# The convolution's second product by tokens, and a written order behind gate and up, in a trunk kernel on one core

## The chip, the cores and the metric

The kernel runs on one core of a Trainium2 chip. The metric is the device time of one launch in microseconds. The engines are named as the profile names them: PE is TensorE's matmul queue and PEld its weight loads, DVE is VectorE, ACT is ScalarE, POOL is GpSimd, SP is SyncE, which here only starts DMAs.

## The reference, cut to what matters

One sequence of 256 tokens with 2048 features (in float32) goes through a convolution layer, a feed-forward of width 5632, one dilated attention layer with shared keys and values, a second feed-forward and a last norm. The change touches the end of the convolution layer and both feed-forwards:

```python
def _conformer_conv(h, w1, b1, dw, dw_b, ln_g, ln_b, w2, b2):
    u = h @ w1 + b1
    a, gate = jnp.split(u, 2, axis=-1)
    u = a * jax.nn.sigmoid(gate)
    u = lax.conv_general_dilated(...) + dw_b      # 31 taps, causal, by feature
    u = jax.nn.silu(_layernorm(u, ln_g, ln_b))
    return u @ w2 + b2

h = h + _conformer_conv(_rmsnorm(h, a_norm_g), ...)
h = h + _swiglu(_rmsnorm(h, ffn_norm_g[0]), w_gate, w_up, w_down)   # (silu(x @ wg) * (x @ wu)) @ wd
```

In the kernel, `z` is the normed and activated input of the product with w2, `hT` the residual h, `x` the input of the following product.

## The kernel before, in words

**Products in three passes.** A float32 product is worked out from two parts of each operand, a rounded high part and the remainder: high by high, high by low, low by high. ACT rounds a weight block (`whi`), DVE or POOL subtracts (`wlo`). Blocks come from HBM by SP's DMAs (`raw`, 512 KB, three buffers), two blocks ahead of use (`emit_block`, `next_block`).

**Two layouts.** *By features*: a 128 x 128 tile of the weight is stationary, the activation moves; `project` and `group` run a wide pass of 512 columns (256 tokens, high and low) and a narrow one of 256. The result has features on partitions. *By tokens*: a tile of the activation is stationary (128 tokens), 512 columns of the weight move, three matmuls of 512 for each pair of k tile and token half (`nat`, called by `two_blocks`). The result has tokens on partitions.

**Couples by seven products.** By tokens, two k tiles, two token halves and two blocks of 512 columns make a 2 x 2 by 2 x 2 block product; an item "S" does it in 7 products instead of 8, from sums of the weights (`emit_sums`, on DVE), sums of the activation (`sum_up`) and four extra banks that `combine` adds up. An item "n" is a plain pair of k tiles for both column blocks. The order of items for a product is a string, such as "nnSnSnSn".

**Around the change.** The convolution layer goes over 16 feature tiles j, 12.5 us each: product with w1 (units u, four blocks each), gate, then the taps, shared among DVE, ACT, POOL and, for the last two tiles, PE. POOL also makes w1's low parts. Behind it stands LayerNorm, whose mean and variance come from PE (`st`), then square root on ACT and reciprocal on DVE (line 721). `centred`, `scaled` and `parted` (lines 697 to 710) make z tile by tile: subtract the mean, multiply, Silu on ACT, then cast to the high part and subtract for the low part. This stands in a `manual_schedule`, that is, ACT, DVE and POOL run in the order written. Elsewhere a scheduler sets the order on each engine ahead of the run; `in_order` and `tc.issue_after` pin an instruction behind another on its engine.

The product with w2 is by features: `project_pair` (lines 399 to 421) does the first two units, with the first four k tiles as native float32 matmuls (line 406) so that it can start before z is cast; `out_proj` does the other six and adds bias and residual (`residual`), sums squares (`Norm.add`, on ACT and POOL) and makes the next x from hT (`split_scaled`). The first feed-forward needs the residual by tokens, so it turns hT by 32 transposes (`turn_over`, line 838) and makes the norm's factor for tokens by eight small matmuls (`Norm.rstd_nat`, line 485).

The output product of the attention (wo) is already by tokens: `out_tokens` adds the product to the token-wise residual, sums squares on ACT (`Tokens.add`) and, through `x_of` and `turn_tiles` (line 876), turns each block of 512 features into x, using the product's own banks. `later(n, fn)` runs fn at the n+1-th following `tick`; a tick is one block of weights.

**Gate and up.** `ffn_hidden` goes over 11 couples of column blocks. Behind each, `hidden` (line 968) adds the combined banks to gate and up on DVE (lines 972, 975), runs Silu on ACT (line 973), multiplies on DVE (line 976), and `turned` (line 986) transposes the result for the down product. Their place among the weight splits is the scheduler's, the splits alone (`split`, line 250) are in a written chain.

[...] By tokens, `first_banks` (three `aux`, one `one`) and `second_banks` (two double `pp`) alternate as the plain banks and as the extra banks of the couples.

Of the kernel before, what the change touches and what calls it, by code (L numbers as in the profile page):

```python
# [9 lines left out]
F32 = mybir.dt.float32  # L10
# [6 lines left out]
P = 128  # L17
D = 2048
S = 256
# [34 lines left out]
SUMS_O, REST_O = 3, (0, 1)  # L54

# [3 lines left out]
for _n, _w in (("a_g", DT), ("b1", 2 * DT), ("dw", DT * TAPS), ("dw_b", DT), ("ln_g", DT), ("ln_b", DT),  # L59
               ("b2", DT), ("kv_g", DT), ("b_g", DT), ("f0_g", DT), ("f1_g", DT), ("eps", 2)):  # L60
    _VEC[_n] = _NV
    _NV += _w
# [34 lines left out]
def trunk(ctx: ExitStack, tc: tile.TileContext, xT, vec, const, w1, w2, wk, wv, wq, wo, wg0, wu0, wd0, wg1, wu1, wd1, fing, out):  # L97
# [126 lines left out]
    last_split = {}  # L224

# [50 lines left out]
    def emit_block():  # L276
# [7 lines left out]
        native = NATIVE if g == 0 and (w is w1 or w is w2 and u < 2) else 0  # L284
# [11 lines left out]
        for s in range(0, gk, step):  # L296
            if with_x:
                load_x(GK * g + s, step)
            part = slice(s, s + step)
            nc.sync.dma_start(raw[:, part, :], src[:, part, :])  # L300
            part = slice(max(s, native), s + step)
            if natural:
                split(hi, lo, raw)
                continue
            if part.start < part.stop:
                nc.scalar.copy(hi[:, part, :], raw[:, part, :])  # L306
                eng = nc.gpsimd if (w is w1 and u > 1) or (w is w2 and u < 2 and (u, g) in ((0, 1), (1, 1), (0, 2))) else nc.vector
                eng.tensor_tensor(out=lo[:, part, :], in0=raw[:, part, :], in1=hi[:, part, :].bitcast(F32), op=ALU.subtract)  # L308
# [90 lines left out]
    def project_pair(w, xf, x, bks):  # L399

        parts = [next_block(w, u, 0, 0)[0] for u in range(2)]
        for s in range(0, GK, 2):
            for bk, raw in zip(bks, parts):
                for kt in (s, s + 1):
                    for m in range(2):
                        nc.tensor.matmul(bk[:, m, 0, :], raw[:, kt, m * P:(m + 1) * P], xf[:, kt, :], start=kt == 0, stop=False,
                                         skip_group_check=True)
            yield
        for g in range(1, DT // GK):
            for u, bk in enumerate(bks):  # L410
                hi, lo = next_block(w, u, g, 0)[1:]
                tiles = [(g * GK + j, j, m, slice(m * P, (m + 1) * P)) for j in range(GK) for m in range(2)]
                for wide in ((True, False), (False, True))[u]:
                    for kt, j, m, ws in tiles:
                        if not wide:
                            nc.tensor.matmul(bk[:, m, 0, :], lo[:, j, ws], x[:, kt, 0, :], start=False, stop=False, skip_group_check=True)
                        else:
                            nc.tensor.matmul(bk[:, m, :, :], hi[:, j, ws], x[:, kt, :, :], start=False, stop=kt == DT - 1,
                                             skip_group_check=True)
                yield  # L420

    def nat(jobs, stop=False):

        for o, xs, hi, _, start in jobs:
            nc.tensor.matmul(o, xs[0], hi, start=start, stop=False, skip_group_check=True)  # L425
            nc.tensor.matmul(o, xs[1], hi, start=False, stop=False, skip_group_check=True)  # L426
# [64 lines left out]
    def residual(bk, u, bias, norm):  # L491

        h2 = hT[:, 2 * u:2 * u + 2, :]
        if bias is None:
            nc.vector.tensor_tensor(out=h2, in0=bk[:, :, 0, :], in1=h2, op=ALU.add)
        else:
            for i in range(2):
                nc.vector.scalar_tensor_tensor(out=h2[:, i, :], in0=bk[:, i, 0, :], scalar=v(bias, 2 * u + i), in1=h2[:, i, :],
                                               op0=ALU.add, op1=ALU.add)
        nc.vector.tensor_tensor(out=h2, in0=bk[:, :, 1, :], in1=h2, op=ALU.add)  # L500
        norm.add(h2)

    def out_proj(w, kt_n, x, bias, g, first=()):

        nx = joined_x()
        norm = Norm()
        for u in range(DT // 2):
            residual(first[u] if u < len(first) else project(w, u, kt_n, x), u, bias, norm)
            for i in (2 * u, 2 * u + 1):
                split_scaled(nx, i, v(g, i))  # L510
        return nx, norm


# [4 lines left out]
    with tc.tile_pool(name="cv", bufs=1) as cv, tc.tile_pool(name="cvu", bufs=1) as cvu:  # L518
# [139 lines left out]
        for j in range(DT):  # L658
            if j != 1:
# [21 lines left out]
        for _ in range(3):  # L681
            emit_block()
# [7 lines left out]
        bks = [bank2(), bank2()]  # L690
        pair = project_pair(w2, cT, z, bks)
        with tc.manual_schedule(engines={mybir.EngineType.Activation, mybir.EngineType.DVE, mybir.EngineType.Pool}):
            mu = cv.tile([P, S], F32, name="mu", tag="shift")
            rl = sp.tile([P, S], F32, name="rstd")
            groups = [(0, 1), (1, 1)] + [(j, 2) for j in range(2, DT, 2)]

            def centred(j, n, eng, m):
                c2 = cT[:, j:j + n, :]
                eng.tensor_tensor(out=c2, in0=c2, in1=_bc(m, n), op=ALU.subtract)

            def scaled(j, n):

                c2 = cT[:, j:j + n, :]
                nc.vector.tensor_tensor(out=c2, in0=c2, in1=_bc(st[:, 1, :], n), op=ALU.mult)
                for q in range(j, j + n):
                    nc.scalar.activation(cT[:, q, :], cT[:, q, :], AF.Silu, bias=v("ln_b", q), scale=v("ln_g", q))

            def parted(j, n):
                nc.vector.tensor_copy(z[:, j:j + n, 0, :], cT[:, j:j + n, :])
                nc.vector.tensor_tensor(out=z[:, j:j + n, 1, :], in0=cT[:, j:j + n, :], in1=z[:, j:j + n, 0, :].bitcast(F32), op=ALU.subtract)  # L710


            nc.scalar.activation(rl, st[:, 0, :], AF.Square)
            nc.scalar.copy(mu, st[:, 0, :])
            centred(*groups[0], nc.vector, st[:, 0, :])
            nc.vector.tensor_tensor(out=rl, in0=st[:, 1, :], in1=rl, op=ALU.subtract)
            nc.scalar.activation(rl, rl, AF.Sqrt, bias=ln_eps)
            centred(*groups[1], nc.vector, st[:, 0, :])
            for j, n in groups[5:]:
                centred(j, n, nc.gpsimd, mu)  # L720
            nc.vector.reciprocal(st[:, 1, :], rl)
            for i, (j, n) in enumerate(groups):
                if 2 <= i < 5:
                    centred(j, n, nc.vector, st[:, 0, :])
                scaled(j, n)
                if j in (1, 2):
                    next(pair)
                if j >= 8:
                    parted(j - 4, 2)
                if j == 10:  # L730
                    next(pair)
                    next(pair)
            emit_block()
            parted(12, 2)
            next(pair)
            parted(14, 2)
            next(pair)
            emit_block()
            emit_block()
            next(pair)  # L740
            next(pair)
            parted(0, 2)
            parted(2, 2)

        x, norm = out_proj(w2, DT, z, "b2", "f0_g", bks)


    def first_banks():

        b = [aux([P, NBV]) for _ in range(3)]  # L750
        return [b[0], b[2]], [b[1], one.tile([P, NBV], F32, name="b", tag="one")]

    def second_banks():
        b = [[a[:, i, :, :].rearrange("p a b -> p (a b)") for i in range(2)] for a in (bank2(), bank2())]
        return [[b[i][t] for i in range(2)] for t in range(2)]

    def wide(a):
        return a.rearrange("p (a b) -> p a b", b=P)

    def sum_up(sums, u, two, h, d):  # L760

        h, d = h.rearrange("p (a b) -> p a b", b=S), wide(d)
        two = two.bitcast(F32)
        nc.vector.tensor_tensor(out=h, in0=two[:, :, 0, :], in1=two[:, :, 1, :], op=ALU.add)
        a11, a21, a12, a22 = (h[:, j, t * P:(t + 1) * P] for j in range(2) for t in range(2))
        for i, a, b, op in ((0, a21, a22, ALU.add), (1, d[:, 0, :], a11, ALU.subtract), (2, a11, a21, ALU.subtract),
                            (3, a12, d[:, 1, :], ALU.subtract)):
            nc.vector.tensor_tensor(out=d[:, i, :], in0=a, in1=b, op=op)
        nc.scalar.copy(sums[:, u, :, 0, :], d)
        nc.vector.tensor_tensor(out=sums[:, u, :, 1, :], in0=d, in1=sums[:, u, :, 0, :].bitcast(F32), op=ALU.subtract)  # L770

    n_used = [0]

    def two_blocks(a, b, items, n_sums, n_rest, act, sums, cs, sum_banks, combine):


        u_sums, u_plain = pairs_of(items, n_sums)
        ab = a, b
# [485 lines left out]
```

## Time and profile before

| what | value |
|---|---|
| median of 3 runs (lowest, highest) | 2128.96 us (2127.24, 2130.54) |
| the profiled execution: its time, its span | 2130.14 us, 2128.4 us |
| convolution layer up to LayerNorm | about 0 to 223 us |
| product with w2 | 229 to 322 us |
| first gate and up | 322 to 797 us |
| product with wo | 1318 to 1409 us |
| second gate and up | 1409 to 1883 us |
| HBM traffic | 194 GB/s over the span |

A row of a timeline or chain starts with its start and its length in microseconds; `x3` merges three instructions; in square brackets stands the engine's idle time before it and what ended it. Matmuls overlap in their pipeline, so a matmul's own duration is longer than the distance from one to the next; that distance is what counts. The page's groups end with busy time, mean nanoseconds of one, and the engine's idle time before them.

### The profile page before, as it was taken

To read this page: it belongs to the slowest core of one execution; us is meant where nothing else is said; L and a number is where in the kernel's file an instruction comes from. 1 tells how busy PE (TensorE), PEld (TensorE's weight loads), DVE (VectorE), ACT (ScalarE), POOL (GpSimd) and SP (SyncE) were. 2 spreads that over 40 slices of the span, in tenths; PEclk is the share of its full clock that TensorE was granted. 3 is DMA by queue.
4 is the path that set the end of the run, shared out by engine and by line. 5 is a ranking of instruction groups with operands and counts; after the bars stand their busy time and mean duration, and the time that the engine had idled before them with its cause. 6 is when DMAs were issued, how large, how long until landed. Compare 5 with 4: busy or idle time off the path is not lost.

```text
span 2128.4 us, 28467 instructions
## 1 busy us (share of the span) xinstructions
PE 2103.3 (99%) x10316; PEld 1775.7 (83%) x10316; DVE 1780.6 (84%) x2431; ACT 1186.4 (56%) x1563; POOL 349.6 (16%) x350
## 2 busy tenths in 40 slices
PE   8999899999999999999999999999999999999998
PEld 8999788888888888888888888888888888878886
DVE  6888876888998998878895687887998899888877
ACT  6665555555555555555654566565555555555453
POOL 5999110000000100000000100000000000000200
PEclk9999999999999999999999999999999999999999
DMA  7555367555655557565656645565655565566664
GB/s 246 186 159 169 97 182 239 177 196 198 209 187 198 198 195 250 189 217 190 224 191 194 215 159 160 196 217 182 212 185 195 197 208 188 198 218 211 208 208 149
DMA packets 116095, 414.84 MB, mean 195 GB/s; under 512 B 13041, under 2 KB 14065, under 8 KB 115953
## 3 DMA queue, kind: packets, MB, share of 16 engines
q1 hardware_dynamic: 84960, 301.82, 43.5%
q0 software_dynamic: 30272, 110.11, 14.9%
q8 instruction: 81, 1.33, 0.3%
q10 hardware_dynamic: 720, 1.07, 0.1%
q14 instruction: 62, 0.50, 0.1%
HBM read 404.57 MB, written 8.39 MB: 194 GB/s over the span
## 4 chain that ended last, share of the span: by engine, by line
PE 87%; DVE 6%; DMA 3%; ACT 2%; issue 2%; POOL 0%; SPq 0%; DVEq 0%; ACTq 0%; POOLq 0%
PE pp L425 11%; PE pp L429 10%; PE pp L426 10%; PE aux L425 9%; PE aux L429 9%; PE aux L426 9%; PE pp L352 7%; PE pp L393 7%; PE pp L356 4%; PE b L429 2%; PE b L425 2%; PE b L426 2%; DVE wlo L250 2%; DVE rooms L259 1%; ACT whi L248 1%
## 5 line engine op out<-in xcount | busy, mean ns | idle before, releaser
L250 DVE TENSOR_TENSOR wlo<-raw,whi 128x1024 fp32r<-128x1024 f32 x360 | 431.5, 1229 | 101.4 <-ACT whi L248 86.4
L248 ACT CAST whi<-raw 128x1024 fp32r<-128x1024 f32 x360 | 369.6, 1050 | 254.8 <-DMA raw<-wd 86.7
L306 ACT CAST whi<-raw 128x1024 fp32r<-128x1024 f32 (+1 forms) x189 | 194.4, 1035 | 169.8 <-PE pp L352 55.1
L248 ACT CAST whi<-rooms 128x1024 fp32r<-128x1024 f32 (+1 forms) x140 | 144.9, 1038 | 219.5 <-DVE rooms L259 184.4
L308 DVE TENSOR_TENSOR wlo<-raw,whi 128x1024 fp32r<-128x1024 f32 (+1 forms) x144 | 177.0, 1245 | 79.7 <-ACT whi L306 65.6
L425 PE MATMUL pp<-whi,x 128*128 128x512 f32 x513 | 201.1, 392 | 0.0
L426 PE MATMUL pp<-whi,x 128*128 128x512 f32 x513 | 199.7, 389 | 0.0
L250 DVE TENSOR_TENSOR wlo<-rooms,whi 128x1024 fp32r<-128x1024 f32 (+1 forms) x140 | 168.4, 1203 | 11.1 <-ACT whi L248 7.6
L239 POOL DMA_DIRECT2D work<-wu x60 | 33.1, 551 | 780.5 <-DVE rooms L259 732.6
L425 PE MATMUL aux<-whi,x 128*128 128x512 f32 x404 | 159.0, 394 | 0.0
L426 PE MATMUL aux<-whi,x 128*128 128x512 f32 x404 | 157.4, 390 | 0.0
L250 DVE TENSOR_TENSOR wlo<-work,whi 128x1024 fp32r<-128x1024 f32 x120 | 114.4, 954 | 42.9 <-ACT whi L248 42.3
L429 PE MATMUL pp<-wlo,x 128*128 128x512 f32 x513 | 149.0, 389 | 0.0
L582 DVE SCALAR_TENSOR_TENSOR aux<-up,vecs,aux 128x256 f32<-128x256 f32 x350 | 140.9, 481 | 1.5 <-ACT aux L580 1.5
L248 ACT CAST whi<-work 128x1024 fp32r<-128x1024 f32 x120 | 95.7, 832 | 75.9 <-DMA work<-wg 36.3
L429 PE MATMUL aux<-wlo,x 128*128 128x512 f32 x404 | 132.5, 390 | 0.5 <-DVE wlo L250 0.5
L425 PEld LDWEIGHTS pp<-whi,x 128*128 128x128 f32 x513 | 96.3, 188 | 22.6 <-DVE hid L989 2.9
L425 PE MATMUL pp<-whi,hid 128*128 128x512 f32 x292 | 113.8, 390 | 1.3 <-DVE hT L842 1.3
L426 PE MATMUL pp<-whi,hid 128*128 128x512 f32 x292 | 113.6, 389 | 0.0
L429 PEld LDWEIGHTS pp<-wlo,x 128*128 128x128 f32 x513 | 96.3, 188 | 20.1
L426 PEld LDWEIGHTS pp<-whi,x 128*128 128x128 f32 x513 | 96.3, 188 | 19.7
L393 PE MATMUL pp<-x,whi 128*128 128x256 f32 x600 | 111.9, 288 | 0.0
(378 smaller groups left out, 5022.5 us busy)
## 6 DMA issues: line engine op xcount, KB each, us to landing
raw<-wd SPq DMA_DIRECT2D x128, 512.0 KB, 4.3
raw<-wg SPq DMA_DIRECT2D x116, 512.0 KB, 4.2
raw<-wu SPq DMA_DIRECT2D x116, 512.0 KB, 3.9
raw<-w SPq DMA_DIRECT2D x75, 512.0 KB, 3.8
work<-wg POOLq DMA_DIRECT2D x60, 512.0 KB, 4.6
work<-wu POOLq DMA_DIRECT2D x60, 512.0 KB, 3.8
t<-wd POOLq DMA_DIRECT2D x48, 512.0 KB, 4.4
raw<-wk SPq DMA_DIRECT2D x32, 512.0 KB, 4.1
```

What stands on the lines that cost most here:

```text
L239: nc.gpsimd.dma_start(places[0][:, 1:3, :], src[1])
L248: made.append(nc.scalar.copy(hi, raw))
L250: made.append(nc.vector.tensor_tensor(out=lo, in0=raw, in1=hi.bitcast(F32), op=ALU.subtract))
L306: nc.scalar.copy(hi[:, part, :], raw[:, part, :])
L308: eng.tensor_tensor(out=lo[:, part, :], in0=raw[:, part, :], in1=hi[:, part, :].bitcast(F32), op=ALU.subtract)
L352: nc.tensor.matmul(bk[:, m, :, :], hi, x[:, k, :, :], start=k == 0, stop=k == kt_n - 1 and turned, skip_group_check=True)
L356: nc.tensor.matmul(bk[:, m, 0, :], lo, x[:, k, 0, :], start=False, stop=k == kt_n - 1 and not turned, skip_group_check=True)
L393: nc.tensor.matmul(bks[u][:, m, :], a[:, j, m * P:(m + 1) * P], b, start=kt == 0 and m == 0 and i == 0, stop=kt == DT - 1 and i == len(pas ...
L425: nc.tensor.matmul(o, xs[0], hi, start=start, stop=False, skip_group_check=True)
L426: nc.tensor.matmul(o, xs[1], hi, start=False, stop=False, skip_group_check=True)
L429: nc.tensor.matmul(o, xs[0], lo, start=False, stop=stop and last[id(o)] == n, skip_group_check=True)
L582: nc.vector.scalar_tensor_tensor(out=acc[i % 2], in0=win, scalar=w, in1=acc[i % 2], op0=ALU.mult, op1=ALU.add)
```

## The change

1. The product with w2 is by tokens: w2 is laid out in blocks of two k tiles by 512 columns, `out_tokens` does it, the first half of the columns with plain items only, the second half with three couples by seven products. The first three blocks' low parts are made on POOL, the others by `split` on DVE.
2. The residual is by tokens from the start: late in the convolution, hT's buffer is filled anew with x by tokens (`xN`, two SP DMAs at j = 9), and b2, spread over the tokens, is added by two accumulating DMAs from POOL at j = 11. The first feed-forward is called with `by_tokens` true and so turns nothing over.
3. z: tiles 0 to 3 in a written order, the rest from the queue of `later`, two tiles every second tick; the reciprocal is copied out of PSUM (`rs`), so that its bank can be used.
4. `nat` does all products with the high activation, then all with the low one. `x_of` does all eight transposes, then the scaling; it runs at `later(2 + 2 * i)` instead of `later(1 + i)`, in the product with wo too.
5. `hidden`: the four sums, the Silus and the products are put into the written chains of DVE and ACT that hold the weight splits.

`sum_up` and the sums' places only change form. The helper functions between `first_banks` and `residual_back` move up in the file.

```diff
+ITEMS_2 = "nnnnnnnn", "nnSnSnSn"
+SUMS_2, REST_2 = 3, (0, 1)
...
-    for g in range(DT // GK):
-        blocks.extend((w2, u, g, GK) for u in range(2))
-    for u in range(2, DT // 2):
-        plan(w2, u, DT)
+    for pair, items in enumerate(ITEMS_2):
+        plan_two((w2, 2 * pair), (w2, 2 * pair + 1), items, items.count("S"), REST_2[pair])
...
-        native = NATIVE if g == 0 and (w is w1 or w is w2 and u < 2) else 0
+        native = NATIVE if g == 0 and w is w1 else 0
+        if w is w2:
+            natural = first_w2[0] <= 0
+            first_w2[0] -= 1
...
-                eng = nc.gpsimd if (w is w1 and u > 1) or (w is w2 and u < 2 and (u, g) in ((0, 1), (1, 1), (0, 2))) else nc.vector
-                eng.tensor_tensor(out=lo[:, part, :], in0=raw[:, part, :], in1=hi[:, part, :].bitcast(F32), op=ALU.subtract)
+                eng = nc.gpsimd if w is w1 and u > 1 or w is w2 else nc.vector
+                made = eng.tensor_tensor(out=lo[:, part, :], in0=raw[:, part, :], in1=hi[:, part, :].bitcast(F32), op=ALU.subtract)
+                if eng is nc.gpsimd:
+                    on_pool.append(made.ins)
...
         for o, xs, hi, _, start in jobs:
             nc.tensor.matmul(o, xs[0], hi, start=start, stop=False, skip_group_check=True)
+        for o, xs, hi, _, start in jobs:
             nc.tensor.matmul(o, xs[1], hi, start=False, stop=False, skip_group_check=True)
...
     def x_of(nx, c, banks, g):
-        for j, b in enumerate(banks):
-            b = turn_tiles(c, j, b)
+        for j, b in enumerate([turn_tiles(c, j, b) for j, b in enumerate(banks)]):
             for a in range(2):
...
-                later(1 + i, lambda c=c, banks=[cs[t][i] for t in range(2)]: x_of(nx, c, banks, lambda j: v(g, j)))
+                later(2 + 2 * i, lambda c=c, banks=[cs[t][i] for t in range(2)]: x_of(nx, c, banks, lambda j: v(g, j)))
...
         def hidden(c, cs, summed):
+            if summed:
+                for i in range(2):
+                    for t in range(2):
+                        with in_order("DVE") as made:
+                            made.append(nc.vector.tensor_tensor(out=q[t][i], in0=cs[t][i], in1=q[t][i], op=ALU.add))
+            for t in range(2):
+                g, r = q[t][0], norm.rn[:, t:t + 1]
+                with in_order("ACT") as made:
+                    made.append(nc.scalar.activation(g, g if summed else cs[t][0], AF.Silu, scale=r))
+                silu.append(made[-1].ins)
+            def product():
+                for t in range(2):
+                    (g, u), r = q[t], norm.rn[:, t:t + 1]
+                    with in_order("DVE") as made:
+                        made.append(nc.vector.scalar_tensor_tensor(out=u, in0=u if summed else cs[t][1], scalar=r, in1=g, op0=ALU.mult, op1=ALU.mult))
+            product()
...
         for j in range(DT):
+            if j == 9:
+                hT = rp.tile([P, DT, S], F32, name="hT", tag="hT")
+                for t in range(2):
+                    nc.sync.dma_start(hT[:, :, t * P:(t + 1) * P], xN[t].rearrange("p (k n) -> p k n", n=P))
+            if j == 11:
+                for t in range(2):
+                    with tc.issue_after(on_pool[-1]):
+                        nc.gpsimd.dma_start(hT[:, :, t * P:(t + 1) * P], b2.rearrange("p (k n) -> p k n", n=P), accum_op=ALU.add)
...
-        for _ in range(3):
-            emit_block()
+        emit_block()
...
             nc.vector.reciprocal(st[:, 1, :], rl)
+            scaled(0, 1, st[:, 1, :])
+            scaled(1, 1, st[:, 1, :])
+            scaled(2, 2, st[:, 1, :])
+            parted(0, 1)
+            parted(1, 1)
+            nc.vector.tensor_copy(rs, st[:, 1, :])
+            begun = parted(2, 2).ins
             emit_block()
+        def prepared(j):
+            with tc.issue_after(begun):
+                if j > 4:
+                    centred(j, 2, nc.vector, mu)
+                scaled(j, 2, rs)
+                parted(j, 2)
+        for j in range(4, DT, 2):
+            later(max(0, j - 6), lambda j=j: prepared(j))
+        for k in range(SUMS_2):
+            later((11, 14, 17)[k], lambda k=k: sum_up(sums, k, z[:, 2 * k:2 * k + 2, :, :], room("sq"), room("sq")))
+        later(12, lambda: load_first_sums(w2, four, *pieces))
+        x, norm = out_tokens(w2, ITEMS_2, REST_2, z, sums, "f0_g", 0)
...
-        hid = ffn_hidden(ff, scratch, wg0, wu0, x, norm, False, 0)
+        hid = ffn_hidden(ff, scratch, wg0, wu0, x, norm, True, 0)
...
+        "xN": np.ascontiguousarray(x[0].reshape(2, P, D)),
+        "b2": np.ascontiguousarray(np.broadcast_to(conv_b2[0], (P, D))),
-        "w2": _blocks(conv_w2[0]),
+        "w2": _blocks(conv_w2[0], GKV, NBV),
```

More of the change, by code (lines that the diff above doesn't have):

```diff
@@ L503, in out_proj, with first_banks, second_banks @@
[L503 to L510, printed above, removed]
-        return nx, norm
+    def first_banks():
+        b = [aux([P, NBV]) for _ in range(3)]
+        return [b[0], b[2]], [b[1], one.tile([P, NBV], F32, name="b", tag="one")]
+    def second_banks():
+        b = [[a[:, i, :, :].rearrange("p a b -> p (a b)") for i in range(2)] for a in (bank2(), bank2())]
+        return [[b[i][t] for i in range(2)] for t in range(2)]
@@ L689, in trunk @@
         z = cv.tile([P, DT, 2, S], F32R, name="z", tag="z")
[L690 to L710 removed]
+        mu = cv.tile([P, S], F32, name="mu", tag="shift")
@@ new lines, in trunk, with centred @@
+        rl = sp.tile([P, S], F32, name="rstd")
+        rs = sp.tile([P, S], F32, name="rstd")
+        spare = cvu.tile([P, DT * (PAD + S)], F32, name="spare", tag="up")
+        four, *pieces = (spare[:, a * NBV:b * NBV].rearrange("p (k n) -> p k n", n=NBV) for a, b in ((0, 4), (4, 6), (6, 8)))
+        sums = [cv.tile([P, 4, 2, P], F32R, name="zsums", tag="prod", bufs=3) for _ in range(SUMS_2)]
+        def centred(j, n, eng, m):
+            c2 = cT[:, j:j + n, :]
+            return eng.tensor_tensor(out=c2, in0=c2, in1=_bc(m, n), op=ALU.subtract)
@@ L733, in trunk @@
-            emit_block()
[L734 to L755, printed above, removed]
```

479 lines of the change are left out of this document (224 added, 255 removed).

## The prediction

> **What bounds the kernel.** I read the page first, then the busy time by windows, then the timeline around the convolution's second product, then the chain of waits.
>
> ```profile
> PE 2103.3 (99%) x10316; PEld 1775.7 (83%) x10316; DVE 1780.6 (84%) x2431; ACT 1186.4 (56%) x1563; POOL 349.6 (16%) x350
> ...
> PE 87%; DVE 6%; DMA 3%; ACT 2%; issue 2%; POOL 0%; SPq 0%; DVEq 0%; ACTq 0%; POOLq 0%
> ```
>
> The matmul queue is busy 99% of the span and owns 87% of the chain. So time falls only if matmul time goes, or one of the few gaps. The one large gap stands just ahead of the changed product:
>
> ```profile
> 223.00:229.00 6.00, 1.05 (x5) 0.49 (x5) 4.12 (x7) 3.39 (x7) 4.36 (x4) 0.84 0.00 0
> 229.00:234.00 5.00, 5.00 (x12) 4.01 (x13) 4.86 (x9) 3.99 (x9) 0.58 (x1) 0.51 0.00 0
> 234.00:239.00 5.00, 5.00 (x24) 4.37 (x24) 4.90 (x10) 3.62 (x8) 0.00 (x0) 1.00 0.00 0
> ```
>
> (Columns: window, length, then busy PE, PEld, DVE, ACT, POOL, granted clock, DMA share, GB/s.) While LayerNorm is worked out, TensorE idles some 5 us, and it then runs at a clock of 0.51 until 234, so 12 matmuls pass in 5 us where 24 pass in the next 5.
>
> **The product's own time.** The timeline brackets it:
>
> ```profile
> 225.92 1.76 DVE L721 RECIPROCAL st<-rstd 128x256 f32<-128x256 f32 x1 [0.25 <-ACT rstd L717]
> 227.72 0.75 DVE L704 TENSOR_TENSOR cT<-cT,st 128x256 f32<-128x256 f32 x2
> 228.18 1.09 ACT L706 ACTIVATE cT<-cT,vecs 128x256 f32<-128x256 f32 x2 [0.98 <-DVE cT L704]
> ...
> 228.83 9.68 PE L406 MATMUL pp<-cT,rawn 128*128 128x256 f32 x32 [4.95 <-ACT cT L706]
> 229.10 0.69 DVE L704 TENSOR_TENSOR cT<-cT,st 128x512 f32<-128x512 f32 x1
> ...
> 232.94 0.42 DVE L709 CAST z<-cT 128x512 fp32r<-128x512 f32 x1
> 233.40 0.69 DVE L710 TENSOR_TENSOR z<-cT,z 128x512 fp32r<-128x512 f32 x1
> ...
> 322.02 0.39 PE L425 MATMUL aux<-whi,x 128*128 128x512 f32 x1
> ```
>
> It runs from 228.83 to gate and up's first matmul at 322.02: 93.2 us. The chain gives the pitch of one matmul:
>
> ```profile
> 307.42 7.28 PE pp L352 x32
> 314.70 3.83 PE pp L356 x32
> ```
>
> 512 columns cost 7.28/32 = 0.2275 us, 256 columns 3.83/32 = 0.120 us. Of the 256 weight tiles (16 by 16), 16 run natively in the 9.68 us above, and 240 cost 0.347 us each, 83.4 us. Together 93.0: the stage is bound by matmuls and has no gap worth naming.
>
> **Term A, the new product: -5.6 us.** Stationary z costs 16 k tiles x 2 token halves x 4 column blocks x 3 passes = 384 matmuls of 512 columns. Each of the three couples takes 7 products in place of 8, hence 3 x 3 = 9 fewer: 375 x 0.2275 = 85.3 us. The cold clock stays: the first matmul comes near 229.4 (term B), full clock came at 234, and of those 4.6 us half is lost, 2.3 us. So 87.6 against 93.2. Of this gain the couples themselves are only 9 x 0.2275 = 2.0 us. The rest is that native matmuls go (9.68 us for 16 tiles that would cost 5.6 in passes, partly because these are the cold ones) and that three full passes cost slightly less than wide plus narrow (0.6825 against 4 x 0.347/2 = 0.694).
>
> [...]
>
> **Term B, the start: +0.5 us.** Before, a native matmul needs only the float value out of ACT (the first of the pair begun at 228.18, done about 228.8). Now VectorE does the scaling of tiles 2 and 3 (0.69 us, begun about 228.4 right behind the pair of 0.75), then the cast of tile 0. A 512-wide cast is 0.42, so half of it is estimated at 0.25: first matmul at about 229.4. Tile 1 follows by some 0.6 us, at half clock about when it is wanted. Bounds: 0.2 (the cast overtakes the scaling) to 1.8 (the whole of tiles 0 and 1 first, 0.42 + 0.69 plus the scaling).
>
> **Term C, the norm: -0.9 us, and the transposes: 0.**
>
> ```profile
> L838 PE MATMUL pp<-cst,hT 128*128 128x128 f32 x32 | 4.8, 271 | 0.0
> L485 PE MATMUL pp<-cst,sqacc 128*128 128x1 f32 x8 | 0.9, 239 | 0.0
> ```
>
> The eight matmuls of L485 go, since the squares are now summed by tokens on ACT. The 32 transposes of turn_over go, but x_of brings 32 of the same form, and the work of that helper in the o product shows the same 271 ns:
>
> ```profile
> L876 PE MATMUL pp<-cst,hT 128*128 128x128 f32 x16 | 2.4, 271 | 0.0
> ```
>
> **Term D, VectorE: 0.** In the product's first half (16 blocks x 12 x 0.2275 = 43.7 us) it has, by the rows above, normalising for z: five pairs of 3 x 0.69 + 0.42 and one without centring, 14.3 us. Then about 15 weight splits of 1.23 (18.4) and two z sums of 0.69 + 1.01 + 0.69 (4.8):
>
> ```profile
> L250 DVE TENSOR_TENSOR wlo<-raw,whi 128x1024 fp32r<-128x1024 f32 x360 | 431.5, 1229 | 101.4 <-ACT whi L248 86.4
> ```
> ```profile
> 330.11 1.01 DVE L768 TENSOR_TENSOR sq<-sq 128x128 f32<-128x128 f32 x4
> ```
>
> Together 37.5 us, 86%. TensorE has stood more without idling:
>
> ```profile
> 560.00:930.00 370.00, 370.00 (x1662) 305.90 (x1661) 322.37 (x372) 201.65 (x232) 31.15 (x50) 1.00 0.62 207
> 1365.00:1410.00 45.00, 45.00 (x207) 37.23 (x207) 41.97 (x51) 27.66 (x40) 3.61 (x6) 1.00 0.57 199
> ```
>
> That is 87% (322.37 of 370) and 93% (41.97 of 45); the second row is the same list of items (nnSnSnSn) in the o product as the second half gets. If that cover fails, each missed split costs up to 1.22 us; I take 0, bounds 0 to +4 (about three splits).
>
> **Term E, x_of two ticks later: +1.0 us.** For the pair's second block it now falls into the first couple, whose banks it still holds. In the o product:
>
> ```profile
> 1371.17 0.60 PE L876 MATMUL pp<-cst,hT 128*128 128x128 f32 x4
> ...
> 1372.21 0.47 ACT L444 ACTIVATE x<-pp,vecs 128x256 fp32r<-128x256 f32 x1
> ...
> 1373.48 0.48 DVE L445 SCALAR_TENSOR_TENSOR x<-pp,vecs,x 128x256 fp32r<-128x256 f32 x1
> ```
>
> From the first transpose to the first bank's second split are about 3 us. Three to six matmuls (0.7 to 1.4 us) can run meanwhile, so up to 2.5 us of wait at each of two places (the new product and o), nothing if the queue has other blocks ready. I take 0.5 each, nearer to nothing, because the feed-forward's own turned transposes hold banks in the same manner in the 370 us window without idle time.
>
> **Term F, the residual's DMAs: 0.** xN is 2 MB on SP's queue, in pieces of 512 B, past the w1 loads; b2 is two accumulating DMAs on POOL, behind a w1 split. POOL is the tight engine there:
>
> ```profile
> 150.00:212.50 62.50, 62.50 (x452) 60.14 (x451) 54.79 (x138) 36.53 (x72) 57.21 (x35) 1.00 0.53 169
> ```
>
> That window is the rest of the convolution after b2's place, five units of 12.5 us. POOL's idle time in it is 62.5 - 57.21 = 5.3 us. The DMA engines are busy 0.53 at 169 GB/s, so some 320 at full share: xN's 2.1 MB take about 7 us of them, where the idle 0.47 leaves 5.9 us in each unit. The nearest prices of an issue on POOL:
>
> ```profile
> L238 POOL DMA_DIRECT2D work<-wg x60 | 43.1, 718 | 11.6 <-PE b L426 6.4 <-DMA residual<-hT 5.2
> L239 POOL DMA_DIRECT2D work<-wu x60 | 33.1, 551 | 780.5 <-DVE rooms L259 732.6
> ```
>
> L238 writes 256 rows where L239 writes 128: 167 ns for 128 more, 1.3 ns each. 2,048 pieces would then cost about 0.55 + 1920 x 1.3 ns = 3.05 us, two of them 6.1; at the other end 1.1. [...] Cover:
>
> ```profile
> 193.88 7.06 POOL L308 TENSOR_TENSOR wlo<-raw,whi 128x1024 fp32r<-128x1024 f32 x3
> ...
> 202.75 0.60 PE L393 MATMUL pp<-x,whi 128*128 128x256 f32 x2
> ```
>
> The first of the three splits ends at about 196.2 and is wanted at 202.75, 6.5 us later. 6.1 us of delay fits under that, and 5.3 of it is made good. The same 7.06/3 = 2.35 us is the price of each of w2's first three low halves, which also go to POOL: the second can be ready about 234 (cast done near 231.4), and is wanted past 236. I take 0; bounds 0 to +4 (6.1 less half the slack, and SP's w1 loads late besides).
>
> **Term G, the fixed order behind gate and up: 0.** Between couples the trace shows this already:
>
> ```profile
> 668.93 1.28 DVE L972 TENSOR_TENSOR work<-pp,work 128x512 f32<-128x512 f32 x2
> 670.13 1.28 DVE L975 TENSOR_TENSOR work<-pp,work 128x512 f32<-128x512 f32 x2
> 672.04 1.41 DVE L976 SCALAR_TENSOR_TENSOR work<-work,rstdn 128x512 f32<-128x512 f32 x2 [0.63 <-ACT work L973]
> 673.37 2.35 DVE L250 TENSOR_TENSOR wlo<-raw,whi 128x1024 fp32r<-128x1024 f32 x2
> ```
> ```profile
> 668.15 1.07 PE L429 MATMUL pp<-wlo,xrest 128*128 128x512 f32 x4
> ...
> 676.31 0.39 PE L429 MATMUL aux<-wlo,x 128*128 128x512 f32 x1
> ```
>
> Gate and up both added, two products, then the splits: what the edit fixes. Queued behind the four sums are the next splits; the first ends about 674.6 and its low half is wanted at 676.31, so 1.7 us are to spare. What can be won is bounded by TensorE's idle time in the two stages:
>
> ```profile
> 322.00:797.00 475.00, 474.45 (x2145) 391.23 (x2144) 416.68 (x474) 264.38 (x304) 43.12 (x67) 1.00 0.60 199
> 1409.00:1883.00 474.00, 472.58 (x2121) 388.71 (x2120) 422.03 (x488) 263.81 (x309) 40.05 (x64) 1.00 0.59 198
> ```
>
> 0.55 + 1.42 = 2.0 us; the other end is rival 2. The new order inside nat (all high activations, then all low) keeps the count and, at 0.2275 either way, costs nothing.
>
> **Sum.** -5.6 + 0.5 - 0.9 + 1.0 = -5.0 us. The profiled execution took 2130.14 us (span 2128.4), 1.18 above the median of the runs, 2128.96. Profiled, the new kernel should take 2125.1; its median 2124.0.
>
> **Rivals.**
> 1. POOL or SP makes the convolution late. For: POOL at 92% (57.21 of 62.5). Against: 6.5 us of slack. With two issues of 6 us each, less 5.3 made good, it is +7: 2124 + 7 = 2131. Chance 0.12.
> 2. Slower: the fixed order leaves VectorE's split late in each of 20 couples with sums. The slack is 1.7 us; if sums and products slip 2.7 us (a queue of two splits ahead of them), each couple waits 1.0 us: +20 - 5, 2144. It decides from (5.0 + 4.3)/20 = 0.47 us a couple. Against: the couple shown above has that order and no wait. Chance 0.10.
> 3. The fixed order does more than what the trace shows already: it ends the 2.0 us of idle time of both gate-and-up stages; and the two x_of wait for nothing. 2124.0 - 1.0 - 2.0 = 2121. Chance 0.13.
> 4. The clock stays half for longer (a later first matmul, or a stall in the first blocks). By the clock column it was half from about 227.1 (0.84 over 6 us) to 233.9, a stretch of 6.8 us. Half that stretch more costs 1.7 us; with VectorE behind by two splits, 2.5 more: 2128. Chance 0.15. [...]
>
> The forecast has 0.50. A measurement of this kernel tells 0.2%, 4.3 us, from no change. Below 2124.7: most of the forecast's lower two thirds and rival 3, 0.48. Above 2133.2: rival 2 and a tail of rival 1, 0.11. Between: 0.41. The range 2120 to 2130.5 leaves out rival 2, most of rival 1 and a little below.
>
> **What would show it.** Right: first 512-wide matmul of the product near 229.4; about 88 us from there to gate and up; no L485, no transposes of turn_over; PE busy in 322 to 797 as before. Wrong: a conv unit longer than 12.5 us behind the b2 issue, POOL issues of 3 us or more with splits late; TensorE waiting for z or wlo in the first eight blocks, or for a bank at the first couple; waits at the ends of couples in the feed-forwards.

## The result

| | us |
|---|---|
| before, median of 4 runs (lowest, highest) | 2128.38 (2127.24, 2130.54) |
| after, median of 4 runs (lowest, highest) | 2115.90 (2114.35, 2117.25) |
| ratio, 95% interval | 0.9942 (0.9929 to 0.9954) |
| profiled execution of after: its time, its span | 2117.25, 2115.4 |
| forecast and range | 2124.0 (2120.0 to 2130.5) |

The kernel gained 12.5 us where 5.0 were forecast; the sign was right, the time lies outside the range. The page of after, busy times and chain of waits:

```profile
PE 2094.6 (99%) x10171; PEld 1764.9 (83%) x10171; DVE 1791.9 (85%) x2465; ACT 1188.0 (56%) x1575; POOL 345.0 (16%) x349
...
PE 94%; DVE 2%; DMA 1%; ACT 1%; issue 1%; SPq 0%; POOL 0%; ACTq 0%; DVEq 0%; POOLq 0%
```

TensorE's share of the chain went from 87% to 94%, VectorE's from 6% to 2%. Four points of the span are some 85 us, far more than was gained, so these shares tell which engine the chain runs through and not what the change is worth. The busy times by windows of after (columns as in the prediction):

```profile
223.00:229.00 6.00, 0.65 (x3) 0.25 (x2) 4.35 (x8) 3.49 (x7) 2.54 (x3) 0.63 0.51 175
229.00:234.00 5.00, 4.80 (x11) 3.79 (x12) 4.93 (x11) 2.98 (x6) 0.00 (x0) 0.50 0.00 0
234.00:239.00 5.00, 5.00 (x22) 4.09 (x21) 4.63 (x7) 3.08 (x6) 0.00 (x0) 0.92 0.72 208
319.00:790.00 471.00, 470.90 (x2118) 388.31 (x2117) 420.44 (x486) 262.66 (x309) 40.07 (x64) 1.00 0.59 200
1403.00:1874.00 471.00, 471.00 (x2120) 388.72 (x2119) 420.29 (x487) 263.28 (x309) 40.07 (x64) 1.00 0.59 199
```

Both gate-and-up stages are now busy to the last tenth of a microsecond. The gap ahead of the product still stands (5.54 us, before 4.95). The table has the time from the first matmul of a stage to the first of the next, read from the traces of one execution each:

| stage | before | after | difference |
|---|---|---|---|
| up to the product with w2 | 228.83 | 229.20 | +0.37 |
| product with w2 | 93.19 | 89.75 | -3.44 |
| first gate and up | 474.73 | 471.41 | -3.32 |
| first down product | 234.84 | 234.84 | 0 |
| attention up to wo | 286.40 | 285.79 | -0.61 |
| product with wo | 91.14 | 92.53 | +1.39 |
| second gate and up | 473.72 | 470.96 | -2.76 |
| second down product and end | 245.52 | 240.96 | -4.56 |

The largest single difference is in the last row, and most of it arises at a place that the prediction doesn't speak of: the start of the second down product. Timeline of before there:

```profile
1882.45 1.23 DVE L250 TENSOR_TENSOR wlo<-raw,whi 128x1024 fp32r<-128x1024 f32 x1 [0.40 <-ACT whi L248]
1883.59 0.68 DVE L972 TENSOR_TENSOR work<-pp,work 128x512 f32<-128x512 f32 x1
...
1885.46 1.05 ACT L248 CAST whi<-raw 128x1024 fp32r<-128x1024 f32 x1 [3.05 <-DVE work L972]
1887.92 1.05 ACT L248 CAST whi<-raw 128x1024 fp32r<-128x1024 f32 x1 [1.41 <-DMA raw<-wd]
1888.88 1.33 ACT L973 ACTIVATE work<-work,rstdn 128x512 f32<-128x512 f32 x2
1889.63 0.75 DVE L976 SCALAR_TENSOR_TENSOR work<-work,rstdn 128x512 f32<-128x512 f32 x1 [4.16 <-ACT work L973]
...
1890.90 1.22 DVE L250 TENSOR_TENSOR wlo<-raw,whi 128x1024 fp32r<-128x1024 f32 x1
...
1892.17 0.50 PE L429 MATMUL aux<-wlo,hid 128*128 128x512 f32 x1 [1.90 <-DVE wlo L250]
```

The gate's sum (line 972) is done by 1884.3, but its Silu (line 973) starts at 1888.88: on ACT it stands behind casts of weights, one of which has still to wait for its block. VectorE has a product (line 976) at its head that needs this Silu and stands 4.16 us; behind it stands the split, and for its low half TensorE waits 1.90 us. Then the clock falls, by windows of before:

```profile
1889.80:1892.80 3.00, 1.10 (x6) 0.58 (x5) 3.00 (x5) 2.83 (x4) 0.00 (x0) 1.00 0.00 0
1892.80:1896.20 3.40, 3.40 (x10) 2.65 (x9) 3.37 (x6) 0.47 (x1) 0.00 (x0) 0.50 0.70 186
```

3.4 us at a clock of 0.50 cost another 1.7 us. The same place in the timeline of after:

```profile
1875.52 2.48 DVE L713 TENSOR_TENSOR work<-pp,work 128x512 f32<-128x512 f32 x4
1876.24 1.34 ACT L717 ACTIVATE work<-work,rstdn 128x512 f32<-128x512 f32 x2 [2.46 <-DVE work L713]
1877.48 1.04 ACT L250 CAST whi<-raw 128x1024 fp32r<-128x1024 f32 x1
1877.91 1.40 DVE L724 SCALAR_TENSOR_TENSOR work<-work,rstdn 128x512 f32<-128x512 f32 x2
1879.08 1.06 ACT L250 CAST whi<-raw 128x1024 fp32r<-128x1024 f32 x1 [0.56 <-DMA raw<-wd]
1879.24 3.49 DVE L252 TENSOR_TENSOR wlo<-raw,whi 128x1024 fp32r<-128x1024 f32 x3
```

The Silus run as soon as the first sum is there, ahead of the casts; the splits start right behind the products, TensorE waits for nothing and keeps its clock (1.00 from 1874 to 1886).

### The profile page after: what moved, and what is told of

Read it like the earlier page. It is cut to its first block, busy times and chain, and to the rows that moved or that the text cites. A ratio compares the mean times of both kernels' runs of the same rounds, so it can differ in the third digit from the quotient of the medians.

```text
span 2115.4 us, 28273 instructions
## 1 busy us (share of the span) xinstructions
PE 2094.6 (99%) x10171; PEld 1764.9 (83%) x10171; DVE 1791.9 (85%) x2465; ACT 1188.0 (56%) x1575; POOL 345.0 (16%) x349
## 4 chain that ended last, share of the span: by engine, by line
PE 94%; DVE 2%; DMA 1%; ACT 1%; issue 1%; SPq 0%; POOL 0%; ACTq 0%; DVEq 0%; POOLq 0%
PE pp L409 12%; PE pp L411 12%; PE pp L414 12%; PE aux L409 10%; PE aux L414 10%; PE aux L411 10%; PE pp L400 8%; PE pp L359 6%; PE pp L363 3%; PE b L409 3%; PE b L411 3%; PE b L414 3%; DVE wlo L252 1%; DVE aux L831 0%; PE pp L736 0%
## 5 line engine op out<-in xcount | busy, mean ns | idle before, releaser
L252 DVE TENSOR_TENSOR wlo<-raw,whi 128x1024 fp32r<-128x1024 f32 x383 | 458.9, 1229 | 99.6 <-ACT whi L250 81.5
L250 ACT CAST whi<-raw 128x1024 fp32r<-128x1024 f32 x383 | 390.9, 1049 | 236.5 <-DMA raw<-wd 76.5
L311 ACT CAST whi<-raw 128x1024 fp32r<-128x1024 f32 (+1 forms) x162 | 166.1, 1032 | 132.8 <-PE pp L400 39.1
L313 DVE TENSOR_TENSOR wlo<-raw,whi 128x1024 fp32r<-128x1024 f32 (+1 forms) x117 | 144.2, 1252 | 66.2 <-ACT whi L311 52.7
L409 PE MATMUL pp<-whi,x 128*128 128x512 f32 x513 | 150.7, 392 | 0.0
L411 PE MATMUL pp<-whi,x 128*128 128x512 f32 x513 | 149.0, 389 | 0.0
L411 PE MATMUL aux<-whi,x 128*128 128x512 f32 x404 | 134.0, 389 | 0.0
L409 PE MATMUL aux<-whi,x 128*128 128x512 f32 x404 | 133.4, 392 | 0.0
L313 POOL TENSOR_TENSOR wlo<-raw,whi 128x1024 fp32r<-128x1024 f32 x45 | 109.4, 2469 | 21.2 <-ACT whi L311 21.2
L359 PE MATMUL pp<-x,whi 128*128 128x512 f32 x448 | 109.8, 393 | 0.0
```

Of the source, the lines that this page charges most:

```text
L250: made.append(nc.scalar.copy(hi, raw))
L252: made.append(nc.vector.tensor_tensor(out=lo, in0=raw, in1=hi.bitcast(F32), op=ALU.subtract))
L313: made = eng.tensor_tensor(out=lo[:, part, :], in0=raw[:, part, :], in1=hi[:, part, :].bitcast(F32), op=ALU.subtract)
L359: nc.tensor.matmul(bk[:, m, :, :], hi, x[:, k, :, :], start=k == 0, stop=k == kt_n - 1 and turned, skip_group_check=True)
```

## The experiments

The theory: about 7 us come from the new product and some 5 from edit 5, and of that edit it is the Silu's place on ACT that counts. The rival: the whole gain is the product's (fewer matmuls, no transposes, another clock), and the order only moves work that had room. Each kernel was timed 5 to 11 times beside before; "difference" is the ratio less one, times 2128.

| kernel | median us | ratio (95%) | difference |
|---|---|---|---|
| new product alone | 2121.10 | 0.9968 (0.9955 to 0.9980) | -6.8 |
| written order alone | 2125.59 | 0.9990 (0.9982 to 0.9999) | -2.1 |
| of it the Silus alone | 2125.21 | 0.9984 (0.9975 to 0.9993) | -3.4 |
| of it VectorE alone | 2130.41 | 1.0010 (1.0001 to 1.0019) | +2.1 |
| after, old `hidden` | 2121.54 | 0.9970 (0.9959 to 0.9980) | -6.4 |
| after, old `nat` | 2116.19 | 0.9946 (0.9932 to 0.9960) | -11.5 |
| after, old `x_of` | 2116.00 | 0.9943 (0.9929 to 0.9957) | -12.1 |
| after, idle matmuls | 2113.48 | 0.9934 (0.9921 to 0.9947) | -14.0 |
| after, no couples | 2118.51 | 0.9961 (0.9948 to 0.9973) | -8.3 |
| after, Silus free | 2122.49 | 0.9980 (0.9971 to 0.9989) | -4.3 |
| product and order | 2116.16 | 0.9950 (0.9938 to 0.9963) | -10.6 |
| after, idle matmuls, old `x_of` in wo | 2116.16 | 0.9948 (0.9935 to 0.9960) | -11.1 |

**New product alone, written order alone, and the order's two halves.** The first is after with the `hidden`, `nat` and `x_of` of before. The second is before with the `hidden` of after. The third and fourth put only the Silus, or only VectorE's sums and products, into the written chains:

```diff
# the Silus alone, in before
-                nc.scalar.activation(g, g if summed else cs[t][0], AF.Silu, scale=r)
+                with in_order("ACT") as made:
+                    made.append(nc.scalar.activation(g, g if summed else cs[t][0], AF.Silu, scale=r))
+                silu.append(made[-1].ins)
```

> The whole change without the written order in hidden, with nat's old order and the old x_of (its place and its form): only the product by tokens and the residual's new way are left. Theory 1 (the surplus over the forecast comes from the written order behind gate and up): -5.5 to -7 us against the kernel before, with the wait of 2.07 us at the start of the second down product and the half clock behind it still there. Theory 2 (the surplus comes from the new product, which shifts every later schedule): -11 to -13 us, and no such wait.

> The kernel before with nothing but the new hidden: sums, Silus and products in the written chains. Theory 1: -6 to -7.5 us: about 0.7 in the first gate and up, 2.8 in the second, and 3.8 at the start of the second down product (a wait of 2.07 us and 1.7 us of half clock behind it). Theory 2: within 1.5 us of the kernel before.

> The kernel before, with only the Silus pinned into ACT's chain of casts; DVE's sums and products stay the scheduler's. Theory 1a (the Silu stood on ACT behind a cast that waits for its DMA, and DVE's product waited for the Silu): most of the gain of order_alone, -4 to -7 us, and no 4 us idle of DVE ahead of the product at the end of the second gate and up. Theory 1b (DVE's own order was at fault): within 1.5 us of the kernel before.

> The kernel before, with only DVE's sums and products in the written chain; the Silus stay where the scheduler puts them. Theory 1a: 0 to -2 us, or even slower, as the splits now queue behind a product that still waits for a late Silu. Theory 1b: -5 to -7 us.

The product alone gives 6.8 us of the 12.5, so the rest is elsewhere. Its trace has the wait at the second down product (1.81 us), but not the half clock that theory 1 expected behind it. The order alone gives 2.1 us, a third of what theory 1 expected, and its Silu half 3.4, short of the 4 to 7 expected; the intervals of these two overlap. VectorE's half is a loss.

In the traces the order alone and the Silus alone take 3.4 and 4.1 us off the second down product and end (242.16 and 241.43 us against 245.52), more than the ratios show. One reason may be the profiled execution of before: it has the half clock there and took 1.8 us more than the median, so not every execution need have it.

In the trace of VectorE alone the larger part of the wait has moved to the first down product, where before had none (0.8 us stay at the second):

```profile
PE pp L429 <- DVE wlo L250: 1.7, 1, 1.7
```

That stage is 236.83 us instead of 234.84: with sums and products ahead of the splits by order, and Silus still behind casts, VectorE's head stands waiting. With the Silus pinned (alone, or with VectorE) TensorE has no wait at the start of either down product.

**After, with one part put back.** Each is after with the `hidden`, the `nat` or the `x_of` (place and form) of before.

```diff
# after, old x_of
-        for j, b in enumerate([turn_tiles(c, j, b) for j, b in enumerate(banks)]):
+        for j, b in enumerate(banks):
+            b = turn_tiles(c, j, b)
...
-                later(2 + 2 * i, lambda c=c, banks=...
+                later(1 + i, lambda c=c, banks=...
```

> The changed kernel with the old hidden (sums, Silus and products where the scheduler puts them); nat and x_of stay new. Theory 1 (the written order): the wait of about 2 us at the start of the second down product comes back, with or without a half clock behind it, and the waits for low halves in the second gate and up: +4 to +6 us over the changed kernel, 2120 to 2122. Theory 3 (nat's order ends the waits inside gate and up; the written order only the one at the down product's start): +2 to +3.7, 2118 to 2119.6.

> The changed kernel with nat's old order (high and low activation in turn for each weight). Theory 3: gate and up get their waits back, 1 to 3 us in each, +3 to +5 over the changed kernel, 2119 to 2121. Theory 1: within 1 us, 2115 to 2117.

> The changed kernel with x_of's old place (later 1 + i) and old form. Term E of the prediction (its banks are wanted while it still holds them): the product with wo falls from 92.5 to 91.2 us, total -1 to -1.5, 2114.5. Theory 4 (the later place frees DVE for the weight splits of the following gate and up): the waits in gate and up come back, +1 to +3.

The old `hidden` brings back 5.6 us by the medians (2121.54 against 2115.90), 6.0 by the ratios, and, in its trace, the 1.90 us wait of before as one of 2.1 us, with a stretch of half clock behind it (a line of its list of waits, and a window):

```profile
PE aux L414 <- DVE wlo L252: 2.1, 1, 2.1
```
```profile
1885.90:1889.30 3.40, 3.40 (x10) 2.63 (x9) 2.84 (x7) 1.10 (x2) 0.00 (x0) 0.50 0.74 235
```

The order inside `nat` is worth nothing that can be measured. Nor does the place of `x_of` show in the total: wo takes 91.11 us with the old place instead of 92.53, but the first gate and up of that execution 472.69 instead of 471.41, since a transpose of the old `x_of` stands waiting there:

```profile
PE pp L617 <- DVE x L430: 1.3, 1, 1.3
```

So the later place costs at one product about what it saves behind the other.

**After, Silus free; product and order.** These test the theory on top of the new product: the first leaves VectorE's chain as in after and gives only the Silus back to the scheduler; the second is before plus edits 1 to 3 and 5, with old `nat` and `x_of`.

> The changed kernel with the gate and up sums and products still in VectorE's written chain, the Silus alone put back to the scheduler's place on ScalarE. If the place of the Silus is what the written order is worth (my theory), the wait of TensorE at the second down product returns: 2119 to 2122, with a Silu behind two casts of weights in the timeline there. If VectorE's order is what counts once the new product stands beside it, it stays at 2116.

> Before plus the new product and the written order behind gate and up, without the new place and form of x_of and without the new order inside nat. If the two parts add as they do on top of one another (2128.4 - 7.1 - 5.6) it gives 2116 and a second gate and up of about 471 us; if x_of or nat is needed for the waits inside the second gate and up to go (the order alone left four of them, 1.9 us), 2118 to 2119 and a stage of 473 us or more.

With free Silus the ratio is 0.9980 instead of after's 0.9942 (2122.49 us). TensorE waits at the start of both down products again; at the first one, as with VectorE alone,

```profile
PE pp L414 <- DVE wlo L252: 1.7, 1, 1.7
```

and the stage takes 236.79 us instead of 234.84. The timeline at the second down product shows why:

```profile
1877.82 2.48 DVE L713 TENSOR_TENSOR work<-pp,work 128x512 f32<-128x512 f32 x4
1878.79 1.05 ACT L250 CAST whi<-raw 128x1024 fp32r<-128x1024 f32 x1 [2.71 <-DMA raw<-wd]
1881.28 1.05 ACT L250 CAST whi<-raw 128x1024 fp32r<-128x1024 f32 x1 [1.43 <-DMA raw<-wd]
1882.23 1.34 ACT L716 ACTIVATE work<-work,rstdn 128x512 f32<-128x512 f32 x2
1882.98 1.42 DVE L722 SCALAR_TENSOR_TENSOR work<-work,rstdn 128x512 f32<-128x512 f32 x2 [2.69 <-ACT work L716]
...
1884.32 3.49 DVE L252 TENSOR_TENSOR wlo<-raw,whi 128x1024 fp32r<-128x1024 f32 x3
...
1885.59 0.50 PE L414 MATMUL aux<-wlo,hid 128*128 128x512 f32 x1 [1.75 <-DVE wlo L252]
```

ACT waits for a block that the Silu has nothing to do with, and the Silu waits behind the cast. This is before's wait again, with VectorE's order fixed: the Silu's place is the cause of the waits at the down products, shown from both sides: pinned alone in before they go, freed alone in after they come. The second kernel comes to 2116.16 (10.6 us by the ratio, against 12.3 of after, with intervals that overlap), so within the noise product and order are all there is. One thing stays open: on before alone the order leaves small waits in the second gate and up, which stays at 473.86 us,

```profile
PE aux L429 <- DVE wlo L250: 1.3, 4, 0.5
```

while with the new product beside it there is none and the stage is 471.10. Why the two need each other there no run settled, nor whether the Silus alone would do beside the new product.

**After, no couples.** All items plain in the product with w2; the sums of z go too.

```diff
-ITEMS_2 = "nnnnnnnn", "nnSnSnSn"
+ITEMS_2 = "nnnnnnnn", "nnnnnnnn"
```

> The changed kernel with plain items only in the convolution's second product (no sums of z, no couples by seven products). If the product is bound by matmuls, 9 more of 0.227 us come back: +2.0 us, about 2118. If VectorE's sums (5 us) and the four extra banks had their own price behind the matmuls, it costs less than +1 us or nothing: 2116 to 2117.

2118.51 is 2.6 us more than after's median (4.0 by the ratios, whose intervals overlap). By windows of this kernel the stage is busy throughout:

```profile
228.40:318.70 90.30, 90.28 (x400) 74.83 (x401) 60.08 (x75) 48.26 (x67) 1.73 (x3) 0.98 0.62 192
```

Half of the time at half clock is lost: 1.42 us here (half until 231.26, first matmul 228.42), 2.78 us in after (half until 234.75, first matmul 229.20). Without it the stage is 88.86 us here and 86.97 in after, 1.9 us apart where 2.0 were expected: the couples bring the matmuls they save, and sums and banks cost nothing that shows.

**After, idle matmuls.** 18 matmuls without use stand between LayerNorm's statistics and the product, to see what the cold clock costs:

```diff
+        idle = bank2()[:, 0, :, :].rearrange("p a b -> p (a b)")
+        with tc.issue_after(last_stat[0]):
+            for i in range(18):
+                nc.tensor.matmul(idle, x[:, 4, 0, 0:P], ready[-1][1][:, 0, :], start=True, stop=True, skip_group_check=True)
```

> The changed kernel with 18 matmuls of 512 columns more, into a bank that nobody reads, placed behind the last statistics matmul and ahead of z's first, so that TensorE idles under 2 us there instead of 5.5. By the granted clock (half from 224.5 to 234.8 in the changed kernel, 5.5 us of it under matmuls): full clock at z's first matmul, the product 2.8 us shorter, 2113. If the clock isn't set by that idle time: 2116, or up to 1 us more where the added matmuls are in the way.

TensorE now idles 1.33 us ahead of the product instead of 5.54, and by windows the clock stays whole where after had 0.63 and 0.50:

```profile
221.90:227.70 5.80, 4.50 (x20) 3.38 (x18) 4.40 (x8) 3.56 (x7) 2.54 (x2) 1.00 0.47 179
227.70:232.70 5.00, 4.96 (x22) 4.06 (x23) 4.95 (x10) 3.21 (x5) 0.00 (x0) 1.00 0.00 0
```

The product with w2 takes 87.11 us instead of 89.75, and the kernel has the lowest median of all, 2113.48, under both kernels of the case; its interval overlaps that of after.

**After, idle matmuls and old x_of in wo.** An attempt at the best of both.

> The changed kernel plus the 18 idle matmuls that keep the clock up, with x_of at its old place and in its old form in the product with wo only. The stage tables give 1.4 us for wo (92.53 against 91.11) beside the 2.4 us of the idle matmuls: 2112. If the old place costs in the second gate and up what it saves in wo, 2113.5 as with the idle matmuls alone.

wo takes 91.13 us, but the kernel isn't faster: 2116.16. In its trace the last down product has a wait of 2.26 us for a sum that stands behind late splits, and half clock behind it. By windows:

```profile
2098.00:2100.80 2.80, 0.54 (x4) 0.12 (x2) 2.77 (x11) 0.00 (x0) 1.59 (x1) 1.00 0.00 0
2100.80:2104.20 3.40, 3.40 (x8) 2.75 (x9) 2.25 (x5) 1.63 (x3) 1.78 (x2) 0.50 0.15 59
```

With the idle matmuls alone that wait is 0.87 us and the clock stays (0.999 over the whole span, 0.998 here). Why the last blocks came later is not settled. One profile can't say whether they do so each time, but all five times (2114.59 to 2116.54) lie above the median with the idle matmuls alone.

## Why the prediction was right or wrong

**Term G was the step that failed: 0 forecast, 5.6 us measured** (after with the old `hidden`). It read one couple in the middle of the first gate and up, found there the order that the edit fixes, and took it for all. Then it bounded the gain by TensorE's idle time in two windows that end with the gate-and-up stages. The work of the last couple runs after that: before's wait, at 1890.3 to 1892.2, lies 7 us behind the end of the second window, 1883, and its half clock behind that. The bound of 2.0 us was broken for this reason: by stages the old `hidden` costs after 4.3 us from the second down product on (245.28 against 240.96; 2.1 of wait and 1.7 of clock are in it), 1.6 us in the second gate and up (472.59 against 470.96) and 0.1 in the first.

The busy row was too coarse as well. A matmul's own 0.39 us is longer than the distance of 0.2275 us to the next, so a start that comes up to 0.16 us late leaves no idle time. In the second gate and up of before, distances from start to start go beyond 0.24 us by 4.5 us in all, in after by 2.0, where the busy row of before has only 1.42 us idle.

The 5.6 us hold beside the new product. On before alone the order gave 2.1, and product and order together gave 3.8 more than the product alone; why the worth of G depends on the rest stays open.

**Rival 3** had the right direction and the same bound, so it stopped at 2121. **Rival 2** had the right danger at the wrong place: VectorE's order alone does make splits late, but chiefly at the first down product (a wait of 1.7 us, the stage 2.0 us longer) and not in 20 couples; the Silus' chain takes it away.

**Terms A, B and C** forecast -6.0 and gave -6.8 with the product alone (2.7 to either side). Of the product's 89.75 us in after, 16 transposes are now inside:

```profile
229.20:319.00 89.80, 2.07 (x16) 1.86 (x16) 0.97 0.54 170
319.00:790.00 471.00, 2.07 (x16) 1.87 (x16) 1.00 0.59 200
```

(Windows of after for line 617 alone: window, length, busy PE and PEld, clock, DMA share and GB/s.) At their pitch of 0.1085 us they are 1.7 us, so the product itself is 88.0; forecast 87.6. The other 16 stay in gate and up, so the move costs nothing, and the eight small matmuls of the norm are gone, as term C has it. Term B, in the timeline of after:

```profile
228.76 0.29 DVE L965 CAST z<-cT 128x256 fp32r<-128x256 f32 x1
...
229.20 1.19 PE L409 MATMUL aux<-whi,z 128*128 128x512 f32 x2 [5.54 <-DVE z L965]
```

The first matmul is at 229.20 (forecast 229.4), the gap ahead of it 0.59 us longer than before (forecast 0.5), the cast of 256 columns 0.29 us (estimate 0.25). The half clock, for which term A counts 2.3 us, takes 2.8 us of the product in after and 1.4 without couples, by where the stretch happens to end; that it came out near is in part luck.

**Term D** held: no wait for z or a split in the product. **Term E** was half right. In wo the waits came where they were forecast, by the list of waits of after in that stage:

```profile
PE aux L414 <- DVE wlo L252: 0.4, 1, 0.4
PE aux L409 <- ACT whi L311: 0.2, 1, 0.2
```

The stage lost 1.39 us (0.5 forecast; 0.6 to 1.7 in the other traces with the new place), and not for want of a bank, as the prediction had it: by these rows PE waited for a cast and a split, which share ACT and DVE with the eight scalings. In the new product PE had no such wait. In the total the term can't be seen (2116.00 with the old `x_of`, 2115.90 with the new, intervals of 1.4 parts in a thousand to either side): what the new place costs in wo it saves in the first gate and up, where the old place makes TensorE wait 1.3 us. The prediction's +1.0 has no such saving in it.

**Term F** held. The two issues of b2 took 2.07 us each, between the bounds of 0.55 and 3.05:

```profile
138.82 4.14 POOL L915 DMA_DIRECT2D hT<-b  x2
```

The row lies nearer to the upper bound. The convolution ends no later, so rival 1 fell. **Rival 4** happened in part: in this execution of after the clock was half from 224.51 to 234.75, 10.2 us instead of 6.8. But the stretch began earlier, and ended only 0.75 us behind the 234 that term A counts with, which is 0.4 us of time.

Together, of the 7.5 us that were missed G has 5.6, A to C have 0.8, and the rest is about what E had put on the other side. Of these shares G's alone is clear of the intervals.

## What to carry to other kernels

An edit that fixes an order pays where the scheduler's order is bad, not where the trace looks typical: search the whole trace for the producer's late consumers, the last turn of the loop and the first blocks of the next stage among them, before its worth is bounded by windows. Look for an engine that serves both transfers and a dependency chain, as ACT here with casts of freshly loaded blocks and Silus: in before a cast stood 1.41 us for its block, the Silu behind it started 4.6 us after its sum was done, and VectorE stood 4.16 us for that Silu. Put the short chain ahead of the casts. When only one of two engines is put in a written order, let it be the one at which the wait begins: on before ACT's alone gained 3.4 us and VectorE's alone cost 2.1, while both together gave no more than ACT's alone.

## What the runs showed of the hardware

In three traces a wait of some 2 us on TensorE cost nearly as much again by the clock. Idle times in front of a matmul of 1.90 (before), 2.1 (old `hidden`) and 2.26 us (the last kernel) were each followed by 3.4 us at a clock of 0.50, that is 1.7 us. One of 1.8 us (product alone) was not, by windows of that kernel:

```profile
1881.60:1884.60 3.00, 1.19 (x6) 0.69 (x5) 3.00 (x4) 2.97 (x4) 0.00 (x0) 1.00 0.00 0
1884.60:1888.00 3.40, 3.40 (x17) 2.79 (x16) 3.37 (x7) 0.29 (x2) 0.00 (x0) 1.00 0.77 173
```

17 matmuls start in these 3.40 us, 10 in those of before. Behind the 1.7 us of VectorE alone matmuls start 0.23 us apart (806.56 to 807.93), and behind the 1.75 us of Silus free 0.23 to 0.24 us apart as far as 1886.87. The wait of 1.66 us of Silus free at the first down product made that stage 2.0 us longer, which leaves no room for 1.7 us of clock.

At the product with w2 the clock was at 0.50 for 6.8 us in before (227.12 to 233.94) and for 10.2 us in after (224.51 to 234.75), with 4.95 and 5.54 us idle in front of the product; with 1.33 us idle (idle matmuls) it stayed at 1.00. What makes a wait cost the clock was not shown: each of these figures is from one execution, and of the waits named above the longest without a loss, 1.8 us, lies close to the shortest with one, 1.90 us.
